# Sums of the next x block on GpSimd instead of VectorE, with the output stores on SyncE's queue

## The chip, the cores and the metric

One core of a Trainium2 chip runs the kernel. The metric is the device time in microseconds (us) of one launch, as the median of several runs; lower is better. The engines are named as in the profile: PE is TensorE (matrix products; PEld is its loading of weights), DVE is VectorE, ACT is ScalarE, POOL is GpSimd, and SP is SyncE, which here only issues DMA transfers.

## The reference

Two matrix products with a bias and a GELU between them, over 16 x 512 = 8192 rows:

```python
batch, m, k, h, n = 16, 512, 768, 3072, 768
y = np.matmul(x, w1) + b1                       # x: 8192 x 768, w1: 768 x 3072
y = 0.5 * y * (1.0 + erf(y / np.sqrt(2.0)))
return np.matmul(y, w2).astype(np.float32)      # w2: 3072 x 768
```

All inputs are float32; the kernel multiplies in bf16 and accumulates in float32.

## The kernel before

**Seven products instead of eight.** Each of the two matrix products is cut into 2 x 2 quarters and computed with Strassen's scheme: seven products M1 to M7 of sums of quarters, and sums of these products. This saves PE an eighth of its work and gives DVE sums to make: of the quarters of w1 and w2 (made once), of x (five sums for each block of rows: M4, M3, M1, M7, M6), and of the hidden layer g.

**Blocks.** The rows are taken in pairs of 384 + 384 (`pairs`), ten blocks of 768 rows, numbered p = 0 to 9, and a last one, p = 10, of 256 + 256. In each block the two row halves are the upper and lower quarters of x. A block has a first layer (x by w1, bias, GELU, into `g`) and a second layer (`g` by w2, into the output). The first layer goes over 12 column pairs j with seven products of three matmuls each (`product1`); block 0 uses plain products instead. The second layer goes over `ns` = 3 row groups of 128 + 128 rows (two in the last block), each with seven products of 12 matmuls (`part2`).

**Evictions.** `evacuate` takes each product out of its PSUM bank in a chain. M4 is copied by ACT to `x1`, M3 is added to it by DVE to make `q`, M1 is copied by ACT to `z`, and then M5, M2, M7 and M6 give the four quarters of the result on DVE, each reading one PSUM operand and one SBUF operand. M5 and M7 accumulate in the bank of M4, and M2 and M6 in that of M3, so PE may start M2 only when `q` has been read out, and M7 only when the quarter from M5 has.

**Sums of g.** `gsum` (L181) makes the sums for the second layer in `st` on DVE, both operands in SBUF, 128 x 1536 in bf16. They are placed between the evictions: those of row group i + 1 are issued while the products of row group i run, the last two (M7 and M6) behind M6 of group i.

**The next x.** As soon as a block's first layer is through, `prepare_x` (L233) brings in the next block's x: six loads of 128 rows with a cast to bf16 on GpSimd's DMA queue into `xb`, which has two buffers, and for each a transposing transfer on SP's queue into `xt`. The loads from the third on wait for a transpose to free a buffer. `sum_x` (L240) makes the five sums of quarters of `xt` into `xft`, which `product1` reads (`moving1`, L151; M2 and M5 read `xt` itself). In the second layer of block p >= 1 the sums for the next block are issued on DVE behind M1, M5, M2 and M7 of the third row group (`xsums`, L533 to L536). For block 1 they are made at its own start instead (L459), because before that the room of `xft` serves to make the forms of w1.

**Queues.** Instructions of an engine are kept in program order (`inorder`), and so are the transfers that it issues. SP issues the loads of w1 forms (`load_slot`, a ring of seven places, each load behind M6 of a column pair), the writes of these forms in block 0 and at the start of block 1, and the transposes. GpSimd issues the loads of x and, in `finish2` (L217), the stores of the output, two for each row group, behind M7 and M6; those of the last block alone go through SP. The output tiles `ot` have four places, so those of the third row group use the places of the first again.

Of the kernel before, what the change touches and what calls it, by code (L numbers as in the profile page):

```python
# [11 lines left out]
ALU = mybir.AluOpType  # L12
# [12 lines left out]
XF = {"M3": 0, "M4": 1, "M1": 2, "M6": 3, "M7": 4}  # L25
# [5 lines left out]
def kernel(  # L31
# [8 lines left out]
    nc = tc.nc  # L40
# [4 lines left out]
    R = B * M  # L45
# [14 lines left out]
    while r < R:  # L60
        w = min(HW, (R - r) // 2)
# [8 lines left out]
    def inorder(ins):  # L70
        return tc.keep_in_program_order(ins)

    def dma(queue, out, in_):
        inorder(queue.dma_start(out=out, in_=in_))  # L74
# [14 lines left out]
    xft = keep.tile([P, 5, KH, HW], BF16, name="xft")  # L89
# [15 lines left out]
    def add(dst, a, b):  # L105
        inorder(nc.vector.tensor_tensor(out=dst, in0=a, in1=b, op=ALU.add))  # L106

    def sub(dst, a, b):
        inorder(nc.vector.tensor_tensor(out=dst, in0=a, in1=b, op=ALU.subtract))  # L109
# [71 lines left out]
    def gsum(m, i, j0=0, j1=HP):  # L181
        dst = st[:, SF[m], j0:j1, :]
        a11, a21 = rows(0, 0, i, j0, j1), rows(0, 1, i, j0, j1)
        a12, a22 = rows(1, 0, i, j0, j1), rows(1, 1, i, j0, j1)
        if m == "M1":
            add(dst, a11, a22)
        elif m == "M5":
            add(dst, a11, a12)
        elif m == "M2":
            add(dst, a21, a22)  # L190
        elif m == "M7":
            sub(dst, a22, a12)
        else:
            sub(dst, a11, a21)
# [17 lines left out]
    def out_tile():  # L212
        nonlocal nout
        nout += 1
        return ot[:, nout % 4, :]

    def finish2(t, m, r0, w, i):  # L217
        queue = nc.sync if r0 + 2 * w == R else nc.gpsimd
        if "oa" not in t and m not in ("M4", "M3", "M1"):
            t["oa"], t["ob"] = out_tile(), out_tile()  # L220
            t["c"] = {"11": t["oa"][:, :NB], "12": t["oa"][:, NB:], "21": t["ob"][:, :NB], "22": t["ob"][:, NB:]}
        evacuate(t, m, NB, t.get("c"))
        if m == "M7":
            dma(queue, out=of[r0 + i * P:r0 + (i + 1) * P, :], in_=t["oa"])
        if m == "M6":
            dma(queue, out=of[r0 + w + i * P:r0 + w + (i + 1) * P, :], in_=t["ob"])


    def place(w, n):
        ns = w // P  # L230
        return n // ns, (n % ns) * P

    def prepare_x(r0, w):  # L233
        for n in range(2 * w // P):
            xb = xbp.tile([P, K], BF16, name="xb")
            dma(nc.gpsimd, out=xb[:], in_=xf[r0 + n * P:r0 + (n + 1) * P, :])
            half, c0 = place(w, n)
            inorder(nc.sync.dma_start_transpose(out=xt[:, :, half, c0:c0 + P], in_=xb[:]))

    def sum_x(k, w):  # L240
        b11, b12 = xt[:, :KH, 0, :w], xt[:, :KH, 1, :w]
        b21, b22 = xt[:, KH:, 0, :w], xt[:, KH:, 1, :w]
        if k == 0:
            sub(xft[:, XF["M4"], :, :w], b11, b21)
        elif k == 1:
            sub(xft[:, XF["M3"], :, :w], b22, b12)
        elif k == 2:
            add(xft[:, XF["M1"], :, :w], b11, b22)
        elif k == 3:
            add(xft[:, XF["M7"], :, :w], b21, b22)  # L250
        else:
            add(xft[:, XF["M6"], :, :w], b11, b12)


    def load_w2(j, n):
# [149 lines left out]
    for p, (r0, w) in enumerate(pairs):  # L405
        ns = w // P
        subs = [dict() for _ in range(ns)]
        most = HP - 2
        nxt = pairs[p + 1] if p + 1 < len(pairs) else None

        def early(i, m, a, b):
            part2(subs[i], m, i, a, b)

        def both(i, a, b, close):
            for m in ("M4", "M3"):
                early(i, m, a, b)
                if close:
                    finish2(subs[i], m, r0, w, i)

        def rest(i, m, after=()):  # L420
            part2(subs[i], m, i, 0, HP)
            finish2(subs[i], m, r0, w, i)
            for f in after:
                f()

        def sums(i, *ms):
            return [lambda m=m: gsum(m, i) for m in ms] if i < ns else []

        def xsums(*ks):
            return [lambda k=k: sum_x(k, nxt[1]) for k in ks] if nxt is not None else []  # L430

        forms = [make_w1] if p == 0 else []

        if p == 0:
            for m in ("M1", "M5", "M2"):
                gsum(m, 0)
                late_w2.pop(0)()
            for f in late_w2:
                f()
            for m in ("M7", "M6"):  # L440
                gsum(m, 0)
            for j in range(HP - 1):
                for i in range(ns):
                    early(i, "M3", j, j + 1)
                for i in range(ns):
                    early(i, "M4", j, j + 1)
            both(0, HP - 1, HP, True)
            both(1, HP - 1, HP, True)
        else:
            js = list(range(PLAIN if p == 1 else 0, HP))  # L450
            if p == 1:
                while made < HP:
                    make_w1()
                for j in range(PLAIN):
                    for hc in (j, HP + j):
                        plain(hc, 0)
                        plain(hc, 1)
                load_raw_slots(PLAIN)
                for k in range(5):  # L459
                    sum_x(k, w)  # L460
            ts = [dict() for _ in range(HP)]

            def step1(s, m):
                if 0 <= s < len(js):
                    product1(ts[s], m, p, js[s], w)

            for s in range(len(js)):
                for d, m in ((2, "M7"), (1, "M5"), (0, "M4"), (2, "M6"), (1, "M2"), (0, "M3"), (0, "M1")):
                    step1(s - d, m)
            last = len(js) - 1  # L470
            step1(last - 1, "M7")
            step1(last, "M5")
            early(0, "M4", 0, 5)
            step1(last - 1, "M6")
            step1(last, "M2")
            gsum("M1", 0, 0, most)
            early(0, "M4", 5, most)
            early(0, "M3", 0, most)
            step1(last, "M7")
            step1(last, "M6")  # L480
            gsum("M5", 0, 0, most)
            early(1, "M4", 0, most)
            early(1, "M3", 0, most)
            both(0, most, HP, True)
            gsum("M1", 0, most, HP)
            gsum("M5", 0, most, HP)
            for m in ("M2", "M7", "M6"):
                gsum(m, 0)

        if nxt is not None:  # L490
            prepare_x(*nxt)
        nload = 0

        def load_raw_slots(plain_done=0):
            nonlocal nload
            while nload < RING:
                k = (nload + FIRST) % RING
                need = {j for j in range(HP)
                        if j // 3 * 2 * GRP < (k + 1) * SLOT and (j // 3 + 1) * 2 * GRP > k * SLOT}
                have = {(PLAIN + n) % HP for n in range(made)}  # L500
                if not need <= have or any(plain_done <= j < PLAIN for j in need):
                    break
                load_slot(nload)
                nload += 1

        def forms(n):
            if p > 0:
                return []

            def f():  # L510
                make_w1()
                load_raw_slots()
            return [f] * n

        rest(0, "M1")
        rest(0, "M5", sums(1, "M1"))
        rest(0, "M2", sums(1, "M5"))
        if p == 0:
            both(2, HP - 1, HP, True)
        rest(0, "M7", sums(1, "M2") + forms(1))  # L520
        rest(0, "M6", sums(1, "M7", "M6"))
        if p > 0:
            both(1, most, HP, True)
        rest(1, "M1", forms(1))
        rest(1, "M5", sums(2, "M1") + forms(1))
        rest(1, "M2", sums(2, "M5"))
        rest(1, "M7", sums(2, "M2"))
        rest(1, "M6", sums(2, "M7", "M6"))
        if ns > 2:
            if p > 0:  # L530
                both(2, 0, HP, True)
            later = p == 0
            rest(2, "M1", forms(1) if later else xsums(0, 1))  # L533
            rest(2, "M5", forms(1) if later else xsums(2))
            rest(2, "M2", forms(1) if later else xsums(3))
            rest(2, "M7", () if later else xsums(4))  # L536
            rest(2, "M6")


# [28 lines left out]
```

## Time and profile before

| what | value |
|---|---|
| runs (three) | 899.54, 901.33, 901.49 us; median 901.33 us |
| profiled execution, span | 897.6 us, 14279 instructions |
| TensorE clock granted | 1.000 |
| ACT busy, idle before copies of x from psx (L99) | 380.4 us; 266.8 us |
| DMA, mean | 165 GB/s; 148.30 MB |
| second layer of block 3 | about 313 to 347 us from the span's start |
| period of a full block, from first transpose to first transpose | 392.20 - 310.30 = 81.9 us |

The span runs from the first to the last instruction of one execution; the times of runs include what lies around it, so the median run is 3.7 us above the span. In the groups of instructions a row has the line, the engine, the operation, output and inputs with their sizes, the count, then busy time in us, mean duration of one in ns, and the engine's idle time before them. The timeline has start and duration in us, the engine, the line, the operation and in brackets the idle time ahead with what ended it; consecutive instructions of one kind are joined. In a helper such as `add` (L106) or `sub` (L109) all instructions have the helper's line, so the tile's name tells what they are: `st<-g` is a sum of g, `xft<-xt` a sum of x, `q<-x,psy` the eviction of M3, `ot<-...` an output quarter of the second layer and `tt<-...` one of the first.

### The profile page before, as it was taken

How to read it: one execution, taken by the hardware profiler on the slowest of the kernel's cores; microseconds unless marked ns; L12 is line 12 of the kernel's file. 1: busy time of each engine (PE TensorE's matmuls, PEld its weight loads, DVE VectorE, ACT ScalarE, POOL GpSimd, SP SyncE). 2: the span in 40 equal slices, each digit the busy share in tenths (PEclk: the TensorE clock that was granted, in tenths of full speed). 3: DMA queues.
4: the chain of work that ended last, by engine and by line, in shares of the span. 5: the costliest groups of instructions: out<-in, count | busy, mean ns of one | idle time of the engine just before them, and what ended most of it. 6: DMA issues, size and time to landing. Idle time of an engine off the chain costs nothing.

```text
span 897.6 us, 14279 instructions
## 1 busy us (share of the span) xinstructions
PE 889.9 (99%) x5627; PEld 544.2 (61%) x5627; DVE 597.1 (67%) x1088; ACT 380.4 (42%) x609; POOL 81.3 (9%) x148
## 2 busy tenths in 40 slices
PE   8999999999999999999999999999999999999998
PEld 5656666666666666666666666666666666666774
DVE  1287776677667676766776676767667766766665
ACT  3542474057217603730571175037306711750460
POOL 6200100100110010001001100100010011001000
PEclk9999999999999999999999999999999999999999
DMA  9997976556736663665557366746645663663411
GB/s 170 206 230 201 377 258 163 122 154 207 162 95 200 197 144 100 205 167 115 175 192 165 94 194 203 141 112 197 167 106 178 205 155 98 194 194 106 146 45 71
DMA packets 89159, 148.30 MB, mean 165 GB/s; under 512 B 50796, under 2 KB 68228, under 8 KB 89092
## 3 DMA queue, kind: packets, MB, share of 16 engines
q1 hardware_dynamic: 65588, 101.77, 37.6%
q0 software_dynamic: 23504, 45.62, 23.0%
q8 instruction: 44, 0.72, 0.3%
q14 instruction: 23, 0.19, 0.1%
HBM read 124.56 MB, written 33.42 MB: 176 GB/s over the span
## 4 chain that ended last, share of the span: by engine, by line
PE 98%; DMA 1%; POOL 0%; issue 0%; ACT 0%; DVE 0%; POOLq 0%
PE psx L205 21%; PE psy L205 21%; PE psx L162 18%; PE psy L162 18%; PE psz L205 7%; PE psz L162 6%; PE psy L312 3%; PE psx L312 3%; DMA st<-in_x_dram 1%; PE psy L375 0%; PE psx L375 0%; PE psz L341 0%; POOL st L74 0%; POOL w1t L74 0%; ACT g L314 0%
## 5 line engine op out<-in xcount | busy, mean ns | idle before, releaser
L162 PEld LDWEIGHTS <-w1t 128*128 128x128 bf16 x2457 | 240.0, 98 | 146.1
L205 PEld LDWEIGHTS <-st 128*128 128x128 bf16 x1920 | 187.6, 98 | 124.4
L99 ACT COPY x<-psx 128x384 f32<-128x384 f32 (+1 forms) x149 | 68.0, 457 | 266.8 <-PE psx L205 191.0
L162 PE MATMUL psx<-xft,w1t 128*128 128x384 bf16 (+1 forms) x702 | 148.6, 321 | 0.0
L162 PE MATMUL psy<-xft,w1t 128*128 128x384 bf16 (+1 forms) x702 | 148.5, 321 | 0.0
L170 ACT ACTIVATE g<-tt,b1t 128x768 bf16<-128x768 f32 (+1 forms) x117 | 106.9, 914 | 86.6 <-DVE tt L109 86.6
L205 PE MATMUL psx<-w2t,st 128*128 128x384 bf16 x768 | 135.3, 326 | 0.0
L205 PE MATMUL psy<-w2t,st 128*128 128x384 bf16 x768 | 135.3, 326 | 0.0
L106 DVE TENSOR_TENSOR q<-x,psy 128x384 f32<-128x384 f32 (+1 forms) x149 | 80.9, 543 | 55.6 <-ACT x L99 40.5
L174 ACT ACTIVATE g<-tt,b1t 128x768 bf16<-128x768 f32 (+1 forms) x117 | 106.7, 912 | 22.6 <-DVE tt L109 22.6
L99 ACT COPY z<-psz 128x384 f32<-128x384 f32 (+1 forms) x149 | 69.8, 468 | 93.6 <-PE psz L205 71.5
L205 PEld LDWEIGHTS <-g 128*128 128x128 bf16 x768 | 75.0, 98 | 50.0 <-issue 0.6
L109 DVE TENSOR_TENSOR tt<-z,psx 128x384 f32<-128x384 f32 (+1 forms) x117 | 63.3, 541 | 51.7 <-PE psx L162 51.7
L109 DVE TENSOR_TENSOR tt<-z,psy 128x384 f32<-128x384 f32 (+1 forms) x117 | 63.3, 541 | 45.9 <-PE psy L162 45.9
L106 DVE TENSOR_TENSOR st<-g 128x1536 bf16<-128x1536 bf16 (+2 forms) x116 | 92.5, 812 | 0.0
L74 POOL DMA_DIRECT2D xb<-in_x_dram x58 | 31.2, 542 | 523.9 <-DMA xt<-xb 515.5
L162 PE MATMUL psy<-xt,w1t 128*128 128x384 bf16 (+1 forms) x351 | 74.3, 321 | 0.0
L162 PE MATMUL psz<-xft,w1t 128*128 128x384 bf16 (+1 forms) x351 | 74.3, 321 | 0.0
L162 PE MATMUL psx<-xt,w1t 128*128 128x384 bf16 (+1 forms) x351 | 74.3, 321 | 0.0
L205 PE MATMUL psx<-w2t,g 128*128 128x384 bf16 x384 | 74.2, 326 | 0.0
L205 PE MATMUL psy<-w2t,g 128*128 128x384 bf16 x384 | 72.9, 326 | 0.3 <-ACT g L314 0.3
L205 PE MATMUL psz<-w2t,st 128*128 128x384 bf16 x384 | 67.7, 326 | 0.0
(53 smaller groups left out, 548.0 us busy)
## 6 DMA issues: line engine op xcount, KB each, us to landing
w1t<-w1f SPq DMA_DIRECT2D x117, 672.0 KB, 4.0
out_dram<-ot POOLq DMA_DIRECT2D x60, 384.0 KB, 2.6
xb<-in_x_dram POOLq DMA_DIRECT2D x58, 192.0 KB, 4.1
w2t<-in_w_dram POOLq DMA_DIRECT2D x8, 576.0 KB, 22.5
w1t<-in_w_dram POOLq DMA_DIRECT2D x7, 576.0 KB, 17.9
w1f<-tt SPq DMA_DIRECT2D x6, 672.0 KB, 4.8
w1f<-xft SPq DMA_DIRECT2D x4, 672.0 KB, 3.6
out_dram<-ot SPq DMA_DIRECT2D x4, 384.0 KB, 2.3
```

Source lines behind the costliest of these rows:

```text
L74: inorder(queue.dma_start(out=out, in_=in_))
L99: inorder(nc.scalar.copy(out=dst, in_=src))
L106: inorder(nc.vector.tensor_tensor(out=dst, in0=a, in1=b, op=ALU.add))
L109: inorder(nc.vector.tensor_tensor(out=dst, in0=a, in1=b, op=ALU.subtract))
L162: inorder(nc.tensor.matmul(out=ps[:, :w], lhsT=forms[:, WF[m], kc, :], rhs=moving1(m, kc, w), start=(kc == 0 and m in ("M1", "M3", "M4")), ...
L170: inorder(nc.scalar.activation(out=g[:, j, :, :w], in_=tj[:, 0:2, :w], func=ACTF.Gelu, bias=b1t[:, j:j + 1], scale=1.0))
L174: inorder(nc.scalar.activation(out=g[:, HP + j, :, :w], in_=tj[:, 2:4, :w], func=ACTF.Gelu, bias=b1t[:, HP + j:HP + j + 1], scale=1.0))
L205: inorder(nc.tensor.matmul(out=ps[:, :NB], lhsT=lhs, rhs=w2t[:, j, WF[m], :], start=(j == 0 and m in ("M1", "M3", "M4")), stop=(j == HP - ...
L312: inorder(nc.tensor.matmul(out=py[:, :HW], lhsT=lhs[:, kc, (j % 3) * P:(j % 3 + 1) * P], rhs=xt[:, kc, half, :], start=(kc == 0), stop=(kc ...
```

## The change

The five sums of x for the blocks from p = 2 on are computed by GpSimd, and issued right behind the x loads of `prepare_x` in program order, ahead of the second layer's remaining products; for block 1 they stay on DVE. All output stores are issued on SP's queue. The interleaving of DVE's x sums with the third row group is dropped.

```diff
     def finish2(t, m, r0, w, i):
-        queue = nc.sync if r0 + 2 * w == R else nc.gpsimd
+        queue = nc.sync
...
-    def sum_x(k, w):
+    def sum_x(k, w, on_vector=False):
         b11, b12 = xt[:, :KH, 0, :w], xt[:, :KH, 1, :w]
         b21, b22 = xt[:, KH:, 0, :w], xt[:, KH:, 1, :w]
-        if k == 0:
-            sub(xft[:, XF["M4"], :, :w], b11, b21)
...
+        m, p, q, op = (("M4", b11, b21, ALU.subtract), ("M3", b22, b12, ALU.subtract), ("M1", b11, b22, ALU.add),
+                       ("M7", b21, b22, ALU.add), ("M6", b11, b12, ALU.add))[k]
+        engine = nc.vector if on_vector else nc.gpsimd
+        inorder(engine.tensor_tensor(out=xft[:, XF[m], :, :w], in0=p, in1=q, op=op))
...
-        def xsums(*ks):
-            return [lambda k=k: sum_x(k, nxt[1]) for k in ks] if nxt is not None else []
...
                 for k in range(5):
-                    sum_x(k, w)
+                    sum_x(k, w, True)
...
         if nxt is not None:
             prepare_x(*nxt)
+            if p > 0:
+                for k in range(5):
+                    sum_x(k, nxt[1])
...
-            later = p == 0
-            rest(2, "M1", forms(1) if later else xsums(0, 1))
-            rest(2, "M5", forms(1) if later else xsums(2))
-            rest(2, "M2", forms(1) if later else xsums(3))
-            rest(2, "M7", () if later else xsums(4))
+            for m in ("M1", "M5", "M2"):
+                rest(2, m, forms(1))
+            rest(2, "M7")
             rest(2, "M6")
```

`forms` gives nothing from block 1 on.

More of the change, by code (lines that the diff above doesn't have):

```diff
@@ L238, in prepare_x @@
             inorder(nc.sync.dma_start_transpose(out=xt[:, :, half, c0:c0 + P], in_=xb[:]))
-    def sum_x(k, w):
+    def sum_x(k, w, on_vector=False):
         b11, b12 = xt[:, :KH, 0, :w], xt[:, :KH, 1, :w]
         b21, b22 = xt[:, KH:, 0, :w], xt[:, KH:, 1, :w]
-        if k == 0:
-            sub(xft[:, XF["M4"], :, :w], b11, b21)
[L245 to L252, printed above, removed]
+        m, p, q, op = (("M4", b11, b21, ALU.subtract), ("M3", b22, b12, ALU.subtract), ("M1", b11, b22, ALU.add),
+                       ("M7", b21, b22, ALU.add), ("M6", b11, b12, ALU.add))[k]
+        engine = nc.vector if on_vector else nc.gpsimd
+        inorder(engine.tensor_tensor(out=xft[:, XF[m], :, :w], in0=p, in1=q, op=op))
     def load_w2(j, n):
```

## The prediction

> **What bounds the kernel now.** I read the shares of the engines first, then stretches of the span, then the timeline of one block, then the groups of instructions that move.
>
> ```profile
> PE 889.9 (99%) x5627; PEld 544.2 (61%) x5627; DVE 597.1 (67%) x1088; ACT 380.4 (42%) x609; POOL 81.3 (9%) x148
> 306.00:348.00 42.00, 42.00 (x260) 25.26 (x259) 26.71 (x41) 5.57 (x9) 4.85 (x9) 1.00 0.51 122
> 347.50:389.00 41.50, 41.50 (x258) 24.91 (x256) 31.37 (x60) 29.87 (x46) 1.63 (x3) 1.00 0.63 197
> ```
>
> The stretches (columns: length, length again as core time, then PE, PEld, DVE, ACT, POOL busy, clock, DMA share, GB/s) are the second and the first layer of a steady block. PE is busy for the whole of both at granted clock 1.00. Over the span PE is idle 897.6 - 889.9 = 7.7 us, and the chain of waits has PE for 98% of it, the rest mostly the first x load. So VectorE work taken away can give back nothing in a steady block: the gain is bounded by those 7.7 us, which lie at the start and the end, where the change touches nothing. What is to be asked is only whether it makes PE wait.
>
> Block 3 (r0 = 2304; its second layer runs from 312 to 347) stands for the others. Times are us from the span's start, then duration.
>
> ```profile
> 310.30 20.34 SPq L238 DMA_TRANSPOSE xt<-xb  x6
> 325.74 0.55 POOL L74 DMA_DIRECT2D xb<-in_x_dram  x1 [2.71 <-issue]
> 332.53 0.95 DVE L106 TENSOR_TENSOR st<-g 128x1536 bf16<-128x1536 bf16 x1
> 334.41 1.82 DVE L109 TENSOR_TENSOR st<-g 128x1536 bf16<-128x1536 bf16 x2
> 337.91 0.56 DVE L106 TENSOR_TENSOR q<-x,psy 128x384 f32<-128x384 f32 x1 [1.68 <-PE psy L205]
> 338.38 1.42 DVE L109 TENSOR_TENSOR xft<-xt 128x1152 bf16<-128x1152 bf16 x2
> 341.54 2.11 PE L205 MATMUL psy<-w2t,st 128*128 128x384 bf16 x12
> 347.39 0.65 PE L162 MATMUL psx<-xft,w1t 128*128 128x384 bf16 x3
> ```
>
> In order: the transposes of the next x; the last x load that GpSimd issues; the sums M2, then M7 and M6, of the third row group's g; the eviction q of its M3; two of the five x sums; PE's M2 product, which adds to the bank that q has just read and so can't start before q; and the next block's first product, M4, which reads the x sums.
>
> **Part 1: the sums leave VectorE.** Blocks 1 to 9 each lose five.
>
> ```profile
> L106 DVE TENSOR_TENSOR xft<-xt 128x1152 bf16<-128x1152 bf16 x27 | 20.1, 749 | 0.0
> L109 DVE TENSOR_TENSOR xft<-xt 128x1152 bf16<-128x1152 bf16 x18 | 12.8, 752 | 0.0
> ```
>
> Of these 45, five belong to block 1's own sums and stay on VectorE; 40 and the five short ones of the last block (0.55 each) move: 40 x 0.75 + 5 x 0.55 = 33 us off VectorE. They stood behind q, where VectorE sat idle until 341.74: worth 0.
>
> **Part 2: the sums on GpSimd.** No row has a two-input sum on GpSimd; the nearest are its small ones at the start.
>
> ```profile
> masks.py:199 POOL TENSOR_SCALAR_AFFINE_SELECT st<-st 128x128 f32<-128x128 f32 x1 | 0.3, 288 | 0.1
> masks.py:197 POOL MEMSET st<- 128x128 f32 x1 | 0.2, 231 | 0.0
> L552 POOL MEMSET const-float32-1.0<- 128x1 f32 x1 | 0.1, 98 | 0.0
> ```
>
> One element takes 98 ns, so 128 written elements cost (231 - 98)/127 = 1.05 ns each and 128 read and written ones (288 - 98)/127 = 1.5 ns. A sum of 1152 then costs from 1.3 us (as a memset) to 3.5 us (two one-input passes); between them I take the middle, 2.4. The Trainium skill, "GPSIMD Engine Reference", section 3.1, lists 4497 ns for a fp32 sum of 2048; scaled to 1152 that is an estimate of 2.5 us, and the sum would not change by it.
>
> *Are they in time?* The M4 sum needs only the first three transposes and follows the last load's issue, at 326.3. The other four need the last transpose: issued at 329.4, landing 2.7 to 3.8 later (least and median for the transposes), 332.1 to 333.2. Four sums in a row end at 332.1 + 4 x 2.4 = 341.7 to 342.8. The next block wants M4 at 347.39, M3 and M1 within 1 us of it, M7 at about 351.3 and M6 at 352.3. Cover 9 us; only above some 4.7 us a sum does the last one come late. Cost 0.
>
> *Do they disturb VectorE?* The sums of g also read two SBUF operands, and nowhere before do the two engines compute at once. The two ends are: no wait at all (0), or each of the two waits until the other's instruction is done. I take the second in order of arrival, as both ask for two operand streams of the same memory, and work it out for block 3. An eviction with one operand in PSUM I take as free of it.
>
> (i) The transpose lands at 332.1, ahead of VectorE's M2 sum. GpSimd M3 332.1 to 334.5; VectorE M2 to 335.45, an eviction to 336.0; GpSimd M1 to 337.85; VectorE M7 to 338.8; GpSimd M7 to 341.2; VectorE M6 to 342.15, q to 342.7. PE wants q at 341.54: it stands 1.2 us. (ii) It lands at 333.2, while VectorE's M2 runs. GpSimd M3 from 333.5 to 335.9, VectorE M7 to 336.85, GpSimd M1 to 339.25, VectorE M6 to 340.2, q to 340.75: 0.8 us in time, no stall. Both phases lie in the measured spread, so I take half: 0.6 us x 8 full blocks = 4.8 us. The last short x has four transposes and shorter sums: 0.
>
> *The same at the M4 sum.* It meets the M7 and M6 sums of the second row group (13.7 to 15.5 us after the block's first transpose). After its last load's issue it starts at 13.5 in block 2, 14.3 in blocks 1, 4 and 5, and at 15.0 or later in the others. In block 2 it goes first: to 15.9, the pair to 17.7, q to 18.3, where PE wants it at 17.6: 0.7 us. In the three others it falls between the two: 0 if VectorE goes straight on, 1.0 us each if not. I count block 2 alone; the bounds are 0 to 3.7 us. With (i) in no block or in all eight, the whole lies between 0 and 9.6 + 3.7 = 13 us; with 3.5 us a sum (i) and the M4 place make 2 to 3 us a block, 16 to 24 us.
>
> A rule of the Trainium skill speaks against this change here: "SBUF — State Buffer", section "Who interferes with whom", has a VectorE instruction with two SBUF inputs and a GpSimd one that reads SBUF exclude one another, whoever issues second waiting for the first one's end. No run so far shows it; by the rule the sum is the one above, without it 0.
>
> **Part 3: the stores on SP.** 60 stores leave GpSimd's queue and stand behind the transposes.
>
> ```profile
> out_dram<-ot POOLq DMA_DIRECT2D x60, 384.0 KB, 2.6
> out_dram<-ot SPq DMA_DIRECT2D x4, 384.0 KB, 2.3
> 326.29 1.09 POOL L74 DMA_DIRECT2D out_dram<-ot  x2
> ```
>
> The first row group's two stores went out at 326.3, behind the x loads; now they follow the last transpose at 330.6 and land by 333.3. Their tiles are written again by the third group's M5 eviction, at 341.7: 8 us of cover. The last two stores issue at about 348, before the next block's first weight load at 353.4 (it waits for PE there): cover 5 us. In block 0 the stores join the queue of the w1 form writes, which wait for VectorE in the same order; those leave between 81 and 105, each from 0.3 us of SP. The next block's first two x loads, issued at 349.0 behind the last stores, now follow the fifth sum at about 342; their transposes come at 392. Cost 0. If the cover were gone, the M5 eviction, and with it PE's M7, would wait for a store.
>
> **Sum.** 897.6 + 4.8 + 0.7 = 903.1 us of span; the median run is 901.33, 3.7 above the profiled span, so 906.8: I say **907**.
>
> **The rivals.** *No wait, or one that the slack takes (33%).* This is the case on the other side, not slower. If the two engines read side by side, or the VectorE pairs go on unbroken (then (i) has M7 and M6 done at 339.7 and q at 340.25), no product waits, and the time is 901.3. For it: q has 341.54 - 338.47 = 3.1 us of slack, evictions 1.4 us. Against: two whole sums of 2.4 already exceed it.
> *GpSimd keeps the memory for its row of four sums, or evictions wait for it too (12%).* Nothing stands between the four. VectorE's M2 then starts at 341.7, an eviction, M7, M6 and q follow: 0.95 + 0.56 + 1.82 + 0.56, q at 345.6, PE 4.1 us late in each of 8 blocks, and in the M4 place 1 more at most: 33 to 41 us, about 938. Against: a queued instruction usually gets its turn between two others.
> *The sums are late (4%).* At 6 us each M6 ends at 333.2 + 24 = 357.2, 5 us after its product wants it: 8 x 5 = 40 us, 941. The rows of GpSimd speak against it by a factor of two.
> *Stores behind a held-up SP queue (3%).* If the transposes ended 10 us later, the M5 eviction would wait 1 to 2 us a block: 8 to 16 us, about 913.
> *Faster by more than 0.2% (3%).* PE's 7.7 idle us would have to shrink by 1.8; I see nothing that does it, save a draw of the runs, which lay 1.95 us apart.
>
> **The numbers.** The forecast has 45%; its own range is 902 to 920, from a stall in one place to 3.5 us a sum. A measurement can tell about 0.2% (1.8 us). Within it lie the 33% and a few of the forecast's smallest stalls, less some drift: 0.34; faster 0.03; slower 0.63. From 900, just under the no-wait time, to 926, the range leaves out the heavy cases (16%) and little else.
>
> **What would show it.** GpSimd rows xft<-xt x45 with 1.3 to 3.5 us each; st<-g on VectorE above 0.95 us where they overlap these; q in the third row group later than 341.5 on block 3's scale, and PE idle before psy of L205, released by VectorE, about 0.6 us a block. I am wrong if st<-g keeps 0.95 us, if PE waits at L162 for the x sums, or if VectorE's ot waits for a store.

## The result, and the profile after

The changed kernel takes 911.31 us (median of runs from 908.96 to 914.62) against 900.68 for the kernel before in the same comparison: a ratio of 1.0118 with a 95% interval from 1.0089 to 1.0146. It is 10.6 us slower, in the direction and by the mechanism of the forecast; the price is about twice that of the forecast's sum.

The first look is at the engines and the groups that the change touched, on the page of the changed kernel (columns as on the page before: count, then busy us, mean ns of one, idle us before them):

```profile
PE 893.4 (98%) x5627; PEld 546.5 (60%) x5627; DVE 633.5 (70%) x1043; ACT 380.5 (42%) x609; POOL 169.7 (19%) x133
L246 POOL TENSOR_TENSOR xft<-xt 128x1152 bf16<-128x1152 bf16 (+1 forms) x45 | 121.2, 2717 | 35.9 <-DMA xt<-xb 35.7
L106 DVE TENSOR_TENSOR st<-g 128x1536 bf16<-128x1536 bf16 (+2 forms) x116 | 114.7, 1003 | 0.3 <-ACT g L308 0.3
L109 DVE TENSOR_TENSOR st<-g 128x1536 bf16<-128x1536 bf16 x64 | 103.4, 1655 | 0.0
```

The two rows of sums of g on the page before:

```profile
L106 DVE TENSOR_TENSOR st<-g 128x1536 bf16<-128x1536 bf16 (+2 forms) x116 | 92.5, 812 | 0.0
L109 DVE TENSOR_TENSOR st<-g 128x1536 bf16<-128x1536 bf16 x64 | 58.2, 951 | 0.0
```

VectorE lost 45 instructions and yet is busy for longer: 633.5 us against 597.1. Some 33 us of x sums went, and 67 came in as longer sums of g (these two rows together, 218.1 us against 150.7): the 64 of L109 take 1655 ns on average, where they took 951. Nothing in their work has changed. On GpSimd a sum lasts 2.7 us on average.

Next, the waits of PE (who waited for what: us in total, times, longest us):

```profile
PE psy L205 <- DVE q L106: 9.6, 11, 1.5
```

Before, PE waited for `q` nowhere. Now M2 of the second layer waits for it in eleven places: two in each of blocks 1 to 5, none in blocks 6 to 8, and one in block 9, where the four shorter sums of the last x meet the M7 and M6 sums of the second row group. Each wait is counted from the modelled end of a matmul; from start to start 0.16 us more is lost, so the eleven cost 9.6 + 11 x 0.16 = 11.3 us. That is the loss: the medians of the runs differ by 10.6 us. The profiled execution is 13.4 us longer than the one before (911.0 against 897.6), and 1.6 us of that lies at the start, ahead of anything that the change touches: the granted clock of the first 20 us was 0.91 there and 1.00 before, and the second layer of block 0 begins at 60.42 us instead of 58.77. Of the other 11.8 us the eleven waits leave 0.5 unexplained.

Block 3 again, in the timeline of the changed kernel (start us, duration us, engine, line, what; in brackets the idle time ahead of it). Its first transpose starts at 315.97 now, 5.67 us later than before:

```profile
315.97 19.04 SPq L238 DMA_TRANSPOSE xt<-xb  x6
330.46 2.40 POOL L246 TENSOR_TENSOR xft<-xt 128x1152 bf16<-128x1152 bf16 x1
336.71 11.48 POOL L246 TENSOR_TENSOR xft<-xt 128x1152 bf16<-128x1152 bf16 x4 [3.85 <-DMA xt<-xb]
329.68 3.99 DVE L109 TENSOR_TENSOR st<-g 128x1536 bf16<-128x1536 bf16 x2
334.19 2.11 PE L205 MATMUL psy<-w2t,st 128*128 128x384 bf16 x12 [0.46 <-DVE q L106]
336.81 3.07 DVE L106 TENSOR_TENSOR st<-g 128x1536 bf16<-128x1536 bf16 x1
340.27 2.65 DVE L106 TENSOR_TENSOR st<-g 128x1536 bf16<-128x1536 bf16 x1
343.31 5.69 DVE L109 TENSOR_TENSOR st<-g 128x1536 bf16<-128x1536 bf16 x2
348.92 0.54 DVE L106 TENSOR_TENSOR q<-x,psy 128x384 f32<-128x384 f32 x1
349.52 2.11 PE L205 MATMUL psy<-w2t,st 128*128 128x384 bf16 x12 [1.51 <-DVE q L106]
```

The pair of sums at the first place, in the kernel before:

```profile
324.01 1.82 DVE L109 TENSOR_TENSOR st<-g 128x1536 bf16<-128x1536 bf16 x2
```

There are two places. In the first, the M4 sum runs alone on GpSimd from 330.46 to 332.86. VectorE's pair (M7 and M6 of the second row group) took 1.82 us before and takes 3.99 now, ending at 333.67, 0.81 after the sum on GpSimd; `q` stands behind the pair, and PE behind `q`. In the second, GpSimd's four sums and VectorE's four take turns: M5 ends at 339.88, M2 at 342.92, the pair at 349.00, and `q`, which was due at some 344.2, just after M3's product, starts at 348.92. Alone the four sums of GpSimd take 4 x 2.36 us; they take 11.48, so they too wait, some 0.7 us in each of three turns. One turn, a sum on each engine, takes 3.04 us: VectorE's four sums end at 339.88, at 342.92 and, for the pair, two turns later at 349.00. The evictions of one PSUM and one SBUF operand keep their 0.55 us, also in the middle of a sum on GpSimd.

### The profile page after: what moved, and what is told of

Same layout as the page of the kernel before. It is cut to its first block, busy times and chain, and to the rows that moved or that the text cites. A ratio compares the mean times of both kernels' runs of the same rounds, so it can differ in the third digit from the quotient of the medians.

```text
span 911.0 us, 14336 instructions
## 1 busy us (share of the span) xinstructions
PE 893.4 (98%) x5627; PEld 546.5 (60%) x5627; DVE 633.5 (70%) x1043; ACT 380.5 (42%) x609; POOL 169.7 (19%) x133
## 5 line engine op out<-in xcount | busy, mean ns | idle before, releaser
L246 POOL TENSOR_TENSOR xft<-xt 128x1152 bf16<-128x1152 bf16 (+1 forms) x45 | 121.2, 2717 | 35.9 <-DMA xt<-xb 35.7
L106 DVE TENSOR_TENSOR st<-g 128x1536 bf16<-128x1536 bf16 (+2 forms) x116 | 114.7, 1003 | 0.3 <-ACT g L308 0.3
L109 DVE TENSOR_TENSOR st<-g 128x1536 bf16<-128x1536 bf16 x64 | 103.4, 1655 | 0.0
L109 DVE TENSOR_TENSOR tt<-z,psx 128x384 f32<-128x384 f32 (+1 forms) x117 | 63.3, 541 | 51.6 <-PE psx L162 51.5
L109 DVE TENSOR_TENSOR tt<-z,psy 128x384 f32<-128x384 f32 (+1 forms) x117 | 63.3, 541 | 45.9 <-PE psy L162 45.9
```

The costliest lines, as they stand in the source:

```text
L246: inorder(engine.tensor_tensor(out=xft[:, XF[m], :, :w], in0=p, in1=q, op=op))
```

## The experiments

The theory on trial is that of **turns**: a sum on GpSimd and a sum of g on VectorE exclude each other for a whole instruction, and the only price is that `q` comes late for M2. All ratios are to the kernel before, with the 95% interval.

| kernel | us | before, same comparison | ratio |
|---|---|---|---|
| the change | 911.3 | 900.7 | 1.0118 (1.0089 to 1.0146) |
| 1 stores alone | 902.1 | 901.1 | 1.0012 (1.0001 to 1.0024) |
| 2 sums held back until `q` | 901.8 | 901.1 | 1.0011 (1.0000 to 1.0021) |
| 3 `q` ahead of the pair | 903.9 | 901.1 | 1.0032 (1.0018 to 1.0047) |
| 4 sums cut in three | 906.9 | 901.1 | 1.0074 (1.0052 to 1.0096) |
| 5 writes in place of the sums | 901.9 | 900.2 | one run |
| 6 one-input copies in place of the sums | 902.1 | 900.2 | one run |
| 7 M3 sum ahead of M4 sum | 904.7 | 900.2 | 1.0052 (1.0035 to 1.0070) |
| 8 sums alone | 929.4 | 900.2 | one run |
| 9 kernels 4 and 7 together | 901.9 | 901.3 | 1.0005 (0.9994 to 1.0016) |
| 10 kernels 3 and 7 together | 904.5 | 901.3 | 1.0031 (1.0020 to 1.0042) |

**1. The stores alone.** The x sums are back on VectorE where they were; only the stores' queue is changed.

```diff
-            if p > 0:
-                for k in range(5):
-                    sum_x(k, nxt[1])
...
+            rest(2, "M1", forms(1) if later else xsums(0, 1))
```

> Stores on SP as in the change, all x sums back on VectorE where they were before. Theory of turns (a GpSimd sum and a VectorE sum of g exclude each other for a whole instruction, and the only price is q coming late for PE's M2): the time is that of the kernel before, 899 to 902 us, and st<-g keeps 0.95 us. Theory that the stores in SP's queue cost: it stays near 911. Side question: the last transpose of a block's x should be issued 17.2 to 17.8 us after the first, as in the changed kernel, and not 17.9 to 19.1 as before, if it is the stores' leaving that brought it forward.

Timeline of SP, and VectorE's groups:

```profile
309.64 18.92 SPq L238 DMA_TRANSPOSE xt<-xb  x6
L109 DVE TENSOR_TENSOR st<-g 128x1536 bf16<-128x1536 bf16 x64 | 58.2, 952 | 0.0
```

The time is 1.0 us above that of the kernel before (interval 0.1 to 2.2 us), the sums of g are back at 952 ns, and PE waits for nothing in a steady block. Executions with the same granted clock agree: at 1.000 the two of this kernel took 899.0 and 899.9 us, and the five of the kernel before 898.4 to 900.3. So the stores cost nothing that can be told. The side question has a yes for the first blocks: in blocks 1 to 5 the six transposes take 18.9 us from the first's start to the last's end on average (18.2 to 19.6), as in the changed kernel (18.8), and not 19.7 as before (19.1 to 20.3). The stores of the first row group used to go out among the last transposes. That this is the reason is not shown: in blocks 6 to 8 the average is 20.0 us with the stores there and without.

**2. The same sums, later.** A small copy on GpSimd reads `q` of the third row group, and the five sums follow it.

```diff
-            if p > 0:
-                for k in range(5):
-                    sum_x(k, nxt[1])
...
                 both(2, 0, HP, True)
+                if nxt is not None:
+                    inorder(nc.gpsimd.tensor_copy(out=gate[:], in_=subs[2]["q"][:, 0:P]))
+                    for k in range(5):
+                        sum_x(k, nxt[1])
```

> The change, but the five GpSimd sums are held back until q of the third row group has been written (a small GpSimd copy reads q ahead of them). Same 45 sums on GpSimd, same stores. Theory of turns: behind q VectorE has no two-input sum left in the block, so nothing is shut out: st<-g back to 0.95 us, GpSimd sums 2.4 us each, M6 done some 12.3 us after q, about 1 us before its product wants it; PE waits for q nowhere, 899 to 902 us. Rival, that 111 us of GpSimd reading slows the memory or the evictions whenever it runs: 908 to 915 still.

Groups of GpSimd and VectorE:

```profile
L247 POOL TENSOR_TENSOR xft<-xt 128x1152 bf16<-128x1152 bf16 x40 | 93.3, 2359 | 0.1
L110 DVE TENSOR_TENSOR st<-g 128x1536 bf16<-128x1536 bf16 x64 | 58.3, 953 | 0.0
```

The same 45 sums, on the same engine, in the same block: 901.8 us, as with the stores alone (902.1). With no sum of g left to meet, both kinds have their lone times, 2.36 us and 0.95 us, and PE waits for neither `q` nor the x sums. So what costs is the meeting, not GpSimd's work as such; the theory of a general slowing falls here.

**3. `q` ahead of the pair.** On VectorE the sums M7 and M6 of the next row group move behind that group's `q`, for the second group and, as shown here, for the third.

```diff
-        rest(1, "M6", sums(2, "M7", "M6"))
+        rest(1, "M6", sums(2, "M7", "M6") if p == 0 else ())
...
                 both(2, 0, HP, True)
+                for f in sums(2, "M7", "M6"):
+                    f()
```

> The change, but on VectorE the sums M7 and M6 of the next row group are issued behind that group's q instead of ahead of it. Theory of turns: st<-g is stretched as before (means over 1.2 us), but q no longer stands behind stretched sums, so PE's waits for q (9.6 us in 11 places) go; at most 0.5 us a block comes back as waits for the quarter from M5, which now stands behind the pair: 900 to 905 us. Rival (a general slowing): near 911.

The sums of g are still long (means of 1168 and 1587 ns), but all waits of PE for `q` are gone. What comes back is as expected, and seen in the waits:

```profile
PE psx L205 <- DVE ot L109: 1.1, 2, 0.9
PE psy L205 <- DVE ot L109: 0.2, 1, 0.2
```

The pair now delays the quarter from M5, for which M7 waits (first row), and once the quarter from M2, for which M6 waits (second row). Of the loss of 10.6 us only 2.8 are left, and nothing but the order on VectorE has changed.

**4. Shorter turns.** Each sum on GpSimd is cut into three of 384 elements.

```diff
-        inorder(engine.tensor_tensor(out=xft[:, XF[m], :, :w], in0=p, in1=q, op=op))
+            for kc in range(KH):
+                inorder(engine.tensor_tensor(out=xft[:, XF[m], kc, :w], in0=p[:, kc], in1=q[:, kc], op=op))
```

> The change, each GpSimd sum cut into three of 384 elements. Theory of turns: the wait of a VectorE sum is at most one third-sum, some 0.9 us instead of 2.4, so st<-g falls to between 1.0 and 1.9 us where they meet, the chain of four sums delays q by about 4 x 0.9 instead of 4 x 2 us, and q is in time: 900 to 903 us. Rival, that the two share the memory's rate so that the whole reading time of GpSimd counts: no less than 911, rather more, as the small sums cost more in all.

Nearly half of the loss is gone (5.7 us are left), though GpSimd computes for longer (0.91 us a piece alone, so 2.7 a sum). But the forecast of 900 to 903 was missed by 4 us. Block 3 shows both halves (timelines of GpSimd, VectorE and PE):

```profile
328.79 2.65 POOL L250 TENSOR_TENSOR xft<-xt 128x384 bf16<-128x384 bf16 x3
334.88 13.32 POOL L250 TENSOR_TENSOR xft<-xt 128x384 bf16<-128x384 bf16 x12 [3.44 <-DMA xt<-xb]
327.50 4.76 DVE L109 TENSOR_TENSOR st<-g 128x1536 bf16<-128x1536 bf16 x2
339.44 2.78 DVE L109 TENSOR_TENSOR st<-g 128x1536 bf16<-128x1536 bf16 x2
332.78 2.11 PE L205 MATMUL psy<-w2t,st 128*128 128x384 bf16 x12 [1.24 <-DVE q L106]
```

In the second place the turns are short: the pair takes 2.78 us instead of 5.69, and PE waits there in no block. In the first place the second sum of the pair is kept out until all three pieces are through (331.44), as if they were one, and the pair takes 4.76 us. By the profile's starts that sum even began first, at 328.37, and the first piece at 328.79. This happens in four of the eight full blocks; they are the four waits for `q` that are left (0.56 to 1.24 us, 4.4 us with the 0.16 of each). In the others a sum of g gets in after one or two pieces. What decides it is open.

**5 and 6. Writing alone, and reading one operand.** In 5, two memsets of the same piece stand for each sum on GpSimd; in 6, a copy of its first operand. Both leave out the x sums of blocks 2 to 10.

```diff
+            for _ in range(2):
+                inorder(engine.memset(xft[:, XF[m], :, :w], 0.0))
```

> In place of each GpSimd sum two memsets of the same piece of xft: GpSimd writes as often and about as long, and reads nothing. The x sums of blocks 2 to 10 are left out. If it is the reading of SBUF by both engines that shuts one out: st<-g keeps 0.95 us and PE waits for q nowhere. If any GpSimd access to SBUF does it: st<-g stretched to 1.2 us and more, waits for q as in the change.

> In place of each GpSimd sum a GpSimd copy of its first operand: one input instead of two. The x sums of blocks 2 to 10 are left out. Reading collides: a VectorE sum of g that meets a copy waits for that copy's end (one copy at most, 1.2 to 1.9 us by the rows of the start), and st<-g is above 0.95 us where they meet. If it takes two inputs on GpSimd too: st<-g keeps 0.95 us.

Groups of kernel 5:

```profile
L250 POOL MEMSET xft<- 128x1152 bf16 x80 | 82.8, 1058 | 2.3
L109 DVE TENSOR_TENSOR st<-g 128x1536 bf16<-128x1536 bf16 x64 | 58.2, 950 | 0.0
```

Groups of kernel 6:

```profile
L249 POOL COPY xft<-xt 128x1152 bf16<-128x1152 bf16 x40 | 59.5, 1521 | 40.5 <-DMA xt<-xb 35.3 <-PE psx L205 5.2
L109 DVE TENSOR_TENSOR st<-g 128x1536 bf16<-128x1536 bf16 x64 | 75.5, 1220 | 0.0
```

The memsets need no transpose, so they run in one row from the M4 sum's place on (in block 3 from 14.5 to 25.1 us after the first transpose) and meet the sums of g of both places. Writing on GpSimd leaves these at 950 ns: no exclusion. One read operand is enough for it: 1220 ns, with single sums up to 2.3 us. A copy is shorter than a sum (the mean of 1521 ns holds waits, too), so `q` is in time and PE waits nowhere for it. This agrees with the Trainium skill, "SBUF — State Buffer", section "Who interferes with whom", which has a VectorE instruction with two SBUF inputs contend with a GpSimd one that reads SBUF and not with one that only writes.

**7. The M4 sum no longer early.** It goes second, so that the first sum on GpSimd waits for the last transpose too.

```diff
-                for k in range(5):
+                for k in (1, 0, 2, 3, 4):
                     sum_x(k, nxt[1])
```

> The change with the M3 sum ahead of the M4 sum on GpSimd, so that all five wait for the last transpose and none meets the pair of the second row group. Theory of turns: the five waits for q of the second group (0.5 us and 0.16 us of pipeline each, 3.3 us in all) are gone; the waits for q of the third group stay between 0 and 1.5 us a block, less than before, since VectorE is no longer late when the four sums begin: 901 to 908 us. If only the third group's place matters: no change from 911.

4.5 us of the loss are left, so 6.1 are gone (the intervals of the two kernels leave this some 3 us either way); the five waits at the first place had cost 3.3 us by themselves. Block 1 of this kernel shows why more than these can go (timelines of GpSimd and VectorE):

```profile
169.10 14.37 POOL L246 TENSOR_TENSOR xft<-xt 128x1152 bf16<-128x1152 bf16 x5 [6.36 <-DVE ot L109]
168.85 0.95 DVE L106 TENSOR_TENSOR st<-g 128x1536 bf16<-128x1536 bf16 x1
173.22 5.69 DVE L109 TENSOR_TENSOR st<-g 128x1536 bf16<-128x1536 bf16 x2
178.84 0.54 DVE L106 TENSOR_TENSOR q<-x,psy 128x384 f32<-128x384 f32 x1
```

VectorE's M5 sum begins 0.25 us before GpSimd's first and keeps its 0.95 us. Three meetings are left (M2, M7 and M6), and `q` ends at 179.38, in time for M2 at 179.87. In block 3 of the changed kernel M5 began 0.10 us after GpSimd's first sum and became the fourth meeting. The same line divides the blocks of the changed kernel itself: in block 7, without a wait in either place, M5 begins at 670.52 and GpSimd's four at 671.42. A loss of 0.6 us in the first place is what had brought M5 behind the transpose. In the profiled execution one wait of 0.4 us is left, in the short block 9, and one of 0.1 us in block 8; it is the fastest of the runs of this kernel (902.64 to 907.22), and where the slower ones wait was not seen.

**8. The sums alone.** The stores stay on GpSimd's queue, and so behind the five sums.

```diff
-        queue = nc.sync
+        queue = nc.sync if r0 + 2 * w == R else nc.gpsimd
```

> GpSimd sums as in the change, but the stores stay on GpSimd's queue, so behind the five sums. Theory: the first group's stores then leave some 12 us after the last transpose and land 2.6 us later, where the M5 eviction of the third group wants their tiles about 10 us after it; VectorE and with it PE's M7 come 3 to 5 us late in each of eight blocks: 930 to 945 us, with VectorE's ot waiting for a store. Rival, that the stores' place is indifferent: 911.

The waits of VectorE:

```profile
DVE ot L109 <- DMA out_dram<-ot: 28.8, 16, 4.7
```

29 us above the kernel before and so some 18 above the change, just below what was expected: the tiles of the first row group are still being stored when the third wants them. VectorE waits 28.8 us for them, and PE feels it in four blocks, in waits for the quarter from M5 of 2.7 to 3.0 us, 12.2 us from start to start. Behind two of these waits the granted clock fell (0.59 over 354 to 358 us and 0.61 over 609 to 613, against 0.99 and 1.00 in the stretches ahead): by these shares some 3 us more. The waits for `q` are as long as in the change (10.9 us against 11.3). Together this is the 15 us by which the two profiled executions differ behind their starts; the rest of the 18 lies at the start and in the draw of a single run. The two parts of the change belong together: the stores' move saves some 15 us.

**9 and 10. Edits together.**

> Sums cut in three and the M3 sum ahead of the M4 sum. What the thirds alone left (906.9 us) stood in the profile in four waits for q of the second row group, where VectorE's M6 sum was kept out by all three pieces of the M4 sum. With that place empty the theory of turns has waits of at most one piece each, and q in time: no PE wait for q, 900 to 903 us. If cutting leaves a cost of its own (more instructions, more reading time): 905 or more still.

> M3 sum ahead of the M4 sum on GpSimd, and VectorE's pair M7, M6 behind q. Theory of turns: the four meetings that are left stand behind q; what may wait is the quarter from M5, which has 1.4 us of slack behind the pair; fewer waits than with either edit alone (903.9 and 904.7): 900 to 903.5 us. If the two edits act on the same waits, the better of the two is all that comes: 903.9.

Kernel 9 is at 901.9 us, with no wait of PE for `q` in its profile: what cutting alone had left stood in the first place, and the longer time on GpSimd (138.4 us of pieces against 121.2 us of sums in the change) costs nothing. Kernel 10 missed its expectation: 904.5 is no better than either edit alone. With M4 behind M3 the turns end later, and the pair behind `q` meets the last of them; the waits that are left are again those for the quarter from M5 (1.08 us in block 6, 0.29 in block 8). With one of 0.19 us in block 9 they make 2.1 us from start to start, of the 3.2 by which the kernel is slower; the rest was not found.

None of these is faster than the kernel before. PE is busy throughout its steady blocks, so the best that any order could do was to lose nothing.

## Why the prediction was right, and where its sum was off

- **PE bounds, so freeing VectorE gains nothing.** Right: 33 us less VectorE work in kernel 2 give 901.8 us.
- **A sum on GpSimd costs 2.4 us.** Right: 2.36 us alone. That the middle between a memset's price and that of two one-input passes hit it is luck: no row spoke for the middle.
- **In time for the next block.** Right: in block 3 the fifth sum ends at 348.19, and M4's product comes at 355.36.
- **Whole-instruction exclusion in order of arrival, with evictions free of it.** Right for whole sums, and shown by kernels 2, 3, 5, 6 and by the ends of the sums. The order of arrival can't be read from the profile's starts alone: in kernels 3, 4, 6 and 8 some sums of g that began up to 0.42 us ahead of GpSimd's instruction by these starts had to wait for its end all the same.
- **Two phases, with and without a wait.** Right in kind: blocks 6 to 8 have none. But the line between the two lay elsewhere (see below), and the price was mis-sized. For the four sums the term was 0.6 us x 8 = 4.8 us, from half of the blocks at 1.2; measured are five blocks at 1.5 us (0.84 to 1.53, and 0.16 each): 7.5 us. For the M4 sum it was 0.7 us, block 2 alone; measured are five waits with 3.3 us. In four of these five GpSimd's sum got in between VectorE's two; the prediction had that case at 0 to 1.0 us, and counted it at 0. The short block was put at 0 and cost 0.6. Together 11.3 us, where the sum had 5.5.
- **Case (i) was priced too high.** It has three meetings and 1.2 us. Blocks 7 and 8 of the changed kernel have these three meetings and no wait. In block 8 of kernel 7 GpSimd's row starts 21.76 us after the first transpose (721.93), just where (i) has it (timelines of GpSimd and PE):

```profile
743.69 13.80 POOL L246 TENSOR_TENSOR xft<-xt 128x1152 bf16<-128x1152 bf16 x5 [5.98 <-PE psx L205]
753.45 2.11 PE L205 MATMUL psy<-w2t,st 128*128 128x384 bf16 x12
```

M2 starts 31.52 us after the first transpose, where it is due at 31.24 (341.54 - 310.30 in the kernel before): 0.28 us late. The prediction let each sum take its whole lone time behind the other, 2.4 + 0.95 = 3.35 us a turn; measured are 3.04, as a shut-out sum ends sooner behind the other's end than its lone time (0.81 us for VectorE's). Three turns make 0.9 us of difference. So that the 4.8 us of the sum lie within a factor of two of the measured 7.5 is luck: the turns were too dear and, as the next point shows, too few.

- **Why twice as much.** The phases were taken from the transposes of the kernel before, but the change moves them: with the stores behind them they end about 0.9 us sooner in blocks 1 to 5 (kernel 1), and block 3, on which the phases were worked out, had the latest of these (20.34 us against 19.7 on average). So in these blocks the four sums began 20.2 to 20.7 us after the first transpose, where 21.8 to 22.9 had been assumed, and met a fourth sum of g, M5. Block 3's M4 sum, too, started at 14.5 us instead of 15.0 or later. And the two places were treated as independent, while a wait in the first pushes M5 into the second (kernel 7).
- **The stores on SP cost nothing.** Right by what can be told (kernel 1), and the cover named for them was real: kernel 8 pays for its loss.
- **The 3.7 us on top of the span.** Each recorded run lies 1.7 to 1.9 us above its own span. The rest of the 3.7 is that the profiled execution before was a short one. The forecast isn't touched, since it counts from the median run.
- **The rivals.** *No wait* holds in blocks 6 to 8 and fails elsewhere. *GpSimd keeps the memory for its row of four, or evictions wait too* fails for whole sums, which took strict turns, and for evictions, which keep their 0.55 us; for the small pieces of kernel 4 it held in the first place of four blocks. *Late sums* and *stores behind a held-up queue* are seen nowhere in the changed kernel.

## What to carry to other kernels

Moving a two-input sum from VectorE to GpSimd doesn't free VectorE if VectorE goes on with other sums from SBUF at that moment: cost every meeting as a wait for the end of the other engine's instruction (here 3.04 us for a turn of two sums that last 2.36 and 0.95 alone), and follow what stands behind the delayed one in its queue. Whether that costs time is settled by order alone: the same 45 sums cost 10.6 us or nothing that can be told, depending on whether the evictions that TensorE waits for stand behind the meetings. When one part of a change moves transfers, take the phases for the other part from where the transfers will be, not from where they were.

## What the runs showed of the hardware that was not expected

- One read operand on GpSimd is enough to shut out a two-input sum on VectorE (up to 2.3 us for one of 0.95), and writing alone is not (0.95 us).
- Turns are strict between whole sums of 2.36 us in the changed kernel, but three pieces of 0.91 us in a row kept VectorE out together in four blocks of kernel 4, a wait of up to 3 us.
- Of four waits of PE of 2.7 to 3.0 us in kernel 8, two were followed by a lower granted clock (0.59 and 0.61 over 4 us) and two were not (1.00 over 695 to 700 and 780 to 786 us).
- The start of an execution varies by itself: over these profiles the second layer of block 0 begins between 57.8 and 61.8 us, with a granted clock of 0.83 to 1.00 in the first 20 us.
